# Seven products in place of eight for most of the second feed-forward matrix, with two weight sums made by DMA in DRAM

## The chip, the cores and the metric

One core of one Trainium2 chip runs the whole program. The metric is the device time of one execution in microseconds, the median of three runs. The profile was taken on one further execution of the same program.

## What is computed

Two encoder layers run over 512 prompt positions and 32 sample positions, 544 columns in all, in float32. Each layer has two feed-forward networks, and those hold most of the matrix work (model width 1024, inner width 2816):

```python
def swiglu(x, w_in, w_out):
    gate, up = jnp.split(x @ w_in, 2, axis=-1)
    return (jax.nn.silu(gate) * up) @ w_out
# in each layer, twice:
x = layer_norm(ALPHA * x + 0.5 * swiglu(x, w_ffn_in, w_ffn_out), ln_g, ln_b)
```

Between the two networks of a layer stands a mixer (pooling, a short convolution and attention) with an input and an output projection. There are four feed-forward networks in all; "first matrix" below is `w_ffn_in`, "second matrix" is `w_ffn_out`.

## The kernel before

**Layout.** Features lie on the 128 partitions, positions on the free axis. A vector of 1024 model features is 8 tiles of 128 x 544, the inner layer is 22 such tiles ("inner features"). The 544 positions are worked in two halves of 272 (`HS`), because a PSUM bank holds 512 float32 values.

**Three matmuls for one.** A float32 value is split into a high and a low part (`whi`, `wlo` for weights; `xh`, `xl` or `hh`, `hl` for activations). ScalarE copies the value to the high part (L172, L287), VectorE subtracts that from the value (L173, L288). One 128 x 128 block on one half then costs three matmuls of 272 columns: high by high, low by high, high by low.

**Weights.** The object `Weights` walks a list of units in the order in which TensorE needs them. SyncE loads a unit from DRAM into a `raw` buffer, ScalarE and VectorE split each stretch of up to 512 columns into a group (`whi`, `wlo`). There are 3 raw buffers of 1024 columns and 10 groups (`W_BUFS`). A group comes free when TensorE has done its last matmul with it, a raw buffer when the last split or sum that reads it is done.

**Seven products (Strassen's scheme in Winograd's form).** Of the first matrix, inner features 3 to 21 are worked by seven block products in place of eight: the blocks are (gate, up) by (first, second half of the model features), and on the other side the two halves of positions. `sums` (L201 to L216) loads four blocks of 128 x 512, makes four sums of them on VectorE (L198) and splits seven results. `Blocks.add` (L313) makes the sums on the activation side. `seven` (L330) runs 84 matmuls for such a unit; its seven products go to three banks in the order a b a c a c a, each followed by a step that reads the bank (`hidden`, L544). Inner features 0 to 2 are worked plainly with 96 matmuls.

**Second matrix.** The inner features are cut into parts of 8, 7 and 7 (`FSPLIT`). When a part's features are there (in truth one feature later, `plan`, L572), each of the 8 output tiles gets a plain product over the part (`mm2`), and `resid` (L444) adds the bank to `y`, once for each half. The last part runs in `out_phase` (L453), which also does the layer norm `LN`: GpSimd sums `acc` (L380, L381), takes a power (`rstd`, L412) and makes the low parts of the new activations (`xl`, L439). `start` (L521) begins the next network's first three units while the norm is still being applied.

**What sets the order.** A list scheduler puts each engine's instructions into one queue by program order, data and free buffers (the layer norm's steps are drawn forward by 300 places). On the chip every engine works through its own queue in that order and waits by semaphores. GpSimd's queue before holds only the layer norm's and the mixer's work: it has no DMA.

## Time and profile before

| | us |
|---|---|
| median of three runs | 2005.07 (2004.09 to 2005.29) |
| profiled execution | 2006.03 |
| its span, first to last instruction | 2004.2 |
| TensorE busy in the span | 1973.7 (98%) |
| VectorE busy | 1449.9 (72%) |
| ScalarE busy | 993.6 (50%) |
| GpSimd busy | 225.6 (11%) |

The span leaves out 1.8 us of the profiled execution, which lies 1.0 us above the median of the runs. The granted clock of TensorE is 0.992 of full speed over the span. The four feed-forward networks lie roughly at 6 to 383, 633 to 1008, 1012 to 1387 and 1626 to 2004 us. A matmul's busy time (288 ns) is longer than the distance between two matmuls, since they are pipelined; the distance is what counts.

### The profile page before, as it was taken

How to read it: one execution, taken by the hardware profiler on the slowest of the kernel's cores; microseconds unless marked ns; L12 is line 12 of the kernel's file. 1: busy time of each engine (PE TensorE's matmuls, PEld its weight loads, DVE VectorE, ACT ScalarE, POOL GpSimd, SP SyncE). 2: the span in 40 equal slices, each digit the busy share in tenths (PEclk: the TensorE clock that was granted, in tenths of full speed). 3: DMA queues.
4: the chain of work that ended last, by engine and by line, in shares of the span. 5: the costliest groups of instructions: out<-in, count | busy, mean ns of one | idle time of the engine just before them, and what ended most of it. 6: DMA issues, size and time to landing. Idle time of an engine off the chain costs nothing.

```text
span 2004.2 us, 38173 instructions
## 1 busy us (share of the span) xinstructions
PE 1973.7 (98%) x15446; PEld 1937.3 (97%) x15446; DVE 1449.9 (72%) x2806; ACT 993.6 (50%) x2000; POOL 225.6 (11%) x214
## 2 busy tenths in 40 slices
PE   9999999999999999999999999999999999999997
PEld 9999999999899999999999999999899999999997
DVE  7958677677658967768798496775865698576676
ACT  6625445465436544535466254454754366355453
POOL 0000000510134000000420000015001330000003
PEclk9999999999899999999999999999999999999999
DMA  6332323142121242323223223232421213323231
GB/s 208 113 102 95 99 83 116 64 144 92 59 81 63 87 123 67 116 85 102 89 73 108 85 93 109 85 106 72 140 98 54 85 50 99 106 85 109 89 98 46
DMA packets 65834, 189.12 MB, mean 94 GB/s; under 512 B 9428, under 2 KB 15188, under 8 KB 65656
## 3 DMA queue, kind: packets, MB, share of 16 engines
q1 hardware_dynamic: 55584, 172.07, 27.4%
q10 hardware_dynamic: 10072, 14.60, 2.3%
q8 instruction: 121, 1.98, 0.4%
q14 instruction: 57, 0.47, 0.1%
HBM read 179.88 MB, written 8.34 MB: 94 GB/s over the span
## 4 chain that ended last, share of the span: by engine, by line
PE 90%; DVE 6%; issue 1%; ACT 1%; DMA 1%; POOL 1%; POOLq 0%; ACTq 0%; DVEq 0%
PE b L341 39%; PE b L255 30%; PE b L259 15%; DVE wlo L173 1%; PE b L778 1%; PE b L777 1%; DVE sum L198 1%; PE b L793 1%; PE b L419 1%; DVE z L431 1%; ACT ya L433 1%; PE b L865 1%; PE b L758 0%; DMA raw<-in_w 0%; PE b L405 0%
## 5 line engine op out<-in xcount | busy, mean ns | idle before, releaser
L172 ACT ACTIVATE whi<-raw 128x512 fp32r<-128x512 f32 (+2 forms) x586 | 357.3, 614 | 495.6 <-PE b L259 299.1
L173 DVE TENSOR_TENSOR wlo<-raw,whi 128x512 fp32r<-128x512 f32 (+2 forms) x586 | 408.8, 700 | 149.0 <-ACT whi L172 144.2
L255 PE MATMUL b<-hh,wlo 128*128 128x272 f32 x1408 | 405.7, 288 | 0.0
L255 PE MATMUL b<-hh,whi 128*128 128x272 f32 x1408 | 405.1, 288 | 0.0
L259 PE MATMUL b<-hl,whi 128*128 128x272 f32 x1408 | 404.7, 287 | 0.0
L255 PE MATMUL b<-xh,whi 128*128 128x272 f32 x1024 | 296.3, 297 | 10.0 <-ACT xh L438 9.1
L172 ACT ACTIVATE whi<-sum 128x512 fp32r<-128x512 f32 x304 | 190.7, 631 | 201.4 <-PE b L259 99.5
L255 PE MATMUL b<-xh,wlo 128*128 128x272 f32 x1024 | 290.1, 290 | 0.1
L173 DVE TENSOR_TENSOR wlo<-sum,whi 128x512 fp32r<-128x512 f32 x304 | 207.8, 689 | 87.4 <-ACT whi L172 80.4
L259 PE MATMUL b<-xl,whi 128*128 128x272 f32 x1024 | 265.7, 290 | 0.0
L255 PEld LDWEIGHTS b<-hh,whi 128*128 128x128 f32 x1408 | 265.0, 188 | 0.0
L255 PEld LDWEIGHTS b<-hh,wlo 128*128 128x128 f32 x1408 | 264.9, 188 | 0.0
L259 PEld LDWEIGHTS b<-hl,whi 128*128 128x128 f32 x1408 | 264.9, 188 | 0.0
L341 PE MATMUL b<-xh,wlo 128*128 128x272 f32 x912 | 262.6, 288 | 0.0
L341 PE MATMUL b<-xh,whi 128*128 128x272 f32 x912 | 262.2, 288 | 0.0
L341 PE MATMUL b<-xl,whi 128*128 128x272 f32 x912 | 261.8, 287 | 0.0
L255 PEld LDWEIGHTS b<-xh,whi 128*128 128x128 f32 x1024 | 195.1, 191 | 14.0 <-ACT xh L438 11.7
L255 PEld LDWEIGHTS b<-xh,wlo 128*128 128x128 f32 x1024 | 195.5, 191 | 0.6 <-DVE wlo L173 0.3
L259 PEld LDWEIGHTS b<-xl,whi 128*128 128x128 f32 x1024 | 182.3, 190 | 0.7 <-issue 0.5
L341 PE MATMUL b<-s56h,whi 128*128 128x272 f32 x608 | 175.4, 289 | 3.3 <-ACT up L552 3.3
L388 POOL TENSOR_TENSOR ya<-ya,shift 128x544 f32<-128x544 f32 x14 | 25.3, 1830 | 1355.4 <-DVE wlo L173 1313.9
L341 PE MATMUL b<-s73h,wlo 128*128 128x272 f32 x608 | 175.3, 288 | 0.0
(208 smaller groups left out, 4248.1 us busy)
## 6 DMA issues: line engine op xcount, KB each, us to landing
raw<-in_w SPq DMA_DIRECT2D x184, 512.0 KB, 3.8
raw<-in_w SPq DMA_DIRECT2D x64, 448.0 KB, 3.3
raw<-in_wi SPq DMA_DIRECT2D x40, 512.0 KB, 3.2
raw<-in_w SPq DMA_DIRECT2D x42, 256.0 KB, 3.3
raw<-in_wo SPq DMA_DIRECT2D x16, 512.0 KB, 3.2
U<-scr ACTq DMA_DIRECT2D x8, 320.0 KB, 3.5
out_nkT<-k ACTq DMA_DIRECT2D x8, 272.0 KB, 2.1
out_nvT<-vT ACTq DMA_DIRECT2D x8, 272.0 KB, 2.2
```

What stands on the lines that cost most here:

```text
L172: S.activation(out=hi, in_=raw, func=AF.Copy)
L173: V.tensor_tensor(out=lo, in0=raw, in1=hi.bitcast(F32), op=ALU.subtract)
L198: V.tensor_tensor(out=r, in0=a, in1=b, op=ALU.add)
L255: PE.matmul(acc[:, :HALF], v, x[k][0][:, HS[h]], start=first and i == 0, stop=False)
L259: PE.matmul(acc[:, :HALF], w.at(k)[0], x[k][1][:, HS[h]], start=False, stop=last)
L341: PE.matmul(acc[:, :HALF], v[:, cs], x, start=opens and j == 0 and m == 0, stop=j == len(xs) - 1 and m == 2, skip_group_check=True)
L388: POOL.tensor_tensor(out=c, in0=c, in1=self.s, op=ALU.subtract)
L419: PE.matmul(b[:, c * CH:(c + 1) * CH], self.rstd[h][:, c:c + 1].to_broadcast([CH, P]), ident[:CH, :CH], start=True, stop=True)
L431: V.tensor_tensor(out=z, in0=c, in1=self.rstd[h], op=ALU.mult)
L433: S.activation(out=c, in_=z, func=AF.Identity, bias=b, scale=g)
L777: PE.matmul(g[:, :w], qc[c][parts[c], qs], kh[parts[c], :w], start=True, stop=False)
L778: PE.matmul(g[:, :w], qc[c][:, qs], kc[c][:, :w], start=False, stop=True)
```

## The change

The second matrix is now cut into parts of 6, 6, 4 and 6 inner features. The first three parts (16 of 22 features) are worked by seven products: the inner features of a part are taken in pairs (even, odd), the output tiles in pairs, the positions in halves. A unit of the second matrix is a pair of output tiles, with blocks of 384 columns (parts of 6) or 256 (the part of 4); it takes 63 or 42 matmuls in place of 72 or 48. Two such units run in turn, product by product (the `while pairs` loop). `resid7` adds each of the seven bank readings to `y`. Every pair of inner features now needs the activation sums of `Blocks.add`. The last part stays plain.

Of a unit's four weight sums, two (named r1 and r3) are made in DRAM: GpSimd issues a DMA that copies two neighbouring blocks into a DRAM buffer and a second DMA that adds two other blocks to it (`accum_op=ALU.add`). The buffers form a ring of 12; in the program's text the copy of a unit is issued 8 units ahead of the loading, the adding 4 units ahead, after a gate that waits for the first inner feature. This holds for all units of the first and the second matrix that are worked by seven products but the first two. SyncE then loads five blocks for a unit in place of four, now into 7 raw buffers of 512 columns. VectorE makes the two other sums.

In numbers, for the whole program: TensorE 15112 to 14728 matmul instructions; VectorE 2808 to 3364; ScalarE 2004 to 2278; GpSimd gains 244 DMAs (122 copies, 122 additions) and one small copy, the gate; SyncE's DMAs go from 384 to 872.

The tiles of the activations move, too: the first four model features and the even features of a part are held as two half tiles (pool tag `xh`, 16 buffers), and pool `xp` goes from 34 to 26 buffers. Two small loads of the bias go from SyncE's queue to ScalarE's. The core of the diff:

```diff
-FSPLIT = (8, 7, 7)
+FSPLIT = (6, 6, 4, 6)
+SUMS_AHEAD = (8, 4)
+SUMS_FROM = 2
-RAW_BUFS = 3
+RAW_BUFS = 7
         def load(self):
             kind, src, n = self.units[self.loaded]
             self.loaded += 1
+            self.sums_ahead()
...
+        def sums_ahead(self):
+            if self.gate is None:
+                return
+            for ahead, todo, step in zip(SUMS_AHEAD, self.todo, (self.copy, self.accumulate)):
+                while todo and todo[0] < self.loaded + ahead:
+                    step(todo.pop(0))
+
+        def copy(self, i):
+            _, src, n = self.units[i]
+            if len(self.ring) < SUMS_AHEAD[0] + 4:
+                t = dram.tile([P, 2 * G], F32, name=f"r13_{len(self.ring)}")
+            else:
+                t = self.ring.pop(0)
+            self.ring.append(t)
+            self.r13[i] = t[:, :2 * n]
+            with tc.issue_after(self.gate.ins):
+                POOL.dma_start(out=self.r13[i], in_=src[:, :2 * n])
+
+        def accumulate(self, i):
+            _, src, n = self.units[i]
+            POOL.dma_start(out=self.r13[i], in_=src[:, n:3 * n], accum_op=ALU.add)
...
-        def sums(self, src):
+        def seven(self, src, n, r13):
+            blocks = [src[:, :n], src[:, 3 * n:], src[:, 2 * n:3 * n]]
+            blocks += [src[:, n:2 * n]] if r13 is None else [r13[:, :n], r13[:, n:]]
+            b11, b21, b22, *b = (self.fetch(v) for v in blocks)
             g11, g21 = self.group(b11), self.group(b21)
-            r1 = self.add(b11, b12)
+            r1, r3 = b if b[1:] else (self.add(b11, b[0]), self.add(b[0], b22))
             r2 = self.add(r1, b22)
-            g2, g1 = self.group(r2), self.group(r1)
-            g3 = self.group(self.add(b12, b22))
-            g22 = self.group(b22)
+            g2, g1, g3, g22 = (self.group(v) for v in (r2, r1, r3, b22))
             return g11, g21, g2, g1, g3, g22, self.group(self.add(r2, b21))
...
+    def resid7(m, alpha):
+        seen = set()
+        def step(i, h, op):
+            def f(acc):
+                c = y[m + i][:, HS[h]]
+                if alpha and (i, h) not in seen:
+                    V.scalar_tensor_tensor(out=c, in0=c, scalar=ALPHA, in1=acc, op0=ALU.mult, op1=op)
+                else:
+                    V.tensor_tensor(out=c, in0=c, in1=acc, op=op)
+                seen.add((i, h))
+            return f
+        add, sub = ALU.add, ALU.subtract
+        return [step(0, 0, add), step(0, 0, add), step(1, 0, sub), step(1, 1, add), step(1, 1, sub), step(1, 0, add),
+                step(0, 1, add)]
...
-                hs.append(new_x("h"))
-                split(sg, hs[-1])
+                n = i - starts[last]
+                if n >= 0:
+                    tail.append(new_x("h") if n else new_b("h"))
+                    split(sg, tail[-1])
+                elif i % 2 == 0:
...
+                    hb.first.append(new_h("h", 1))
+                    split_half(sg, hb.first[-1], 0)
+                    held = sg
+                else:
+                    hb.second.append(new_x("h"))
+                    split(sg, hb.second[-1])
+                    hb.add(held, sg, new_x)
                 if i == 0:
+                    if W.gate is None:
+                        W.gate = POOL.tensor_copy(out=small("gate", 1), in_=sg[:, :1])
                     W.ahead(3)
...
-            for m in range(NK):
-                acc = run(mm2(W.get(), part, range(n)))
-                for h in range(2):
-                    resid(m, acc[h], h, i == 0)
+            for m in range(0, NK, 4):
+                pairs = [seven(W.get(), parts[i], resid7(m + j, i == 0)) for j in (0, 2)]
+                while pairs:
+                    pairs = [p for p in pairs if next(p, pairs) is not pairs]
```

**The order at two places.** First GpSimd, where the first layer's mixer ends and its second feed-forward network starts; `rstd` is the norm's power, once for each half, `xl` the low part of an activation tile. Before:

```order
L381 TENSOR_TENSOR acc_7261<-acc_7261,sq 128x544 [waits Activation_49,Pool_49]
L412 TENSOR_TENSOR rstd<-var,mhalf 68x4 [waits DVE_49]
L439 TENSOR_TENSOR xl<-ya,xh 128x272 [waits PE_49,Activation_49] x8
L412 TENSOR_TENSOR rstd<-var,mhalf 68x4 [waits DVE_49]
L439 TENSOR_TENSOR xl<-ya,xh 128x272 [waits Activation_49] x8
L388 TENSOR_TENSOR ya<-ya,shift 128x544 [waits DVE_49,Activation_49]
```

After, at the same place (`r_5` is slot 5 of the DRAM ring, L219 the copy, L223 the addition; the DMAHW semaphores are those of loads from SyncE's and ScalarE's queues, the DMASW ones those of GpSimd's own DMAs):

```order
L458 TENSOR_TENSOR rstd<-var,mhalf 68x4 [waits DVE_49]
L485 TENSOR_TENSOR xl<-ya,xh 128x272 [waits PE_49,Activation_49] x8
L458 TENSOR_TENSOR rstd<-var,mhalf 68x4 [waits DVE_49]
L219 DMA r_5_453<-in_w 128x1024 [waits DMAHW1_49,DMAHW0_49]
L485 TENSOR_TENSOR xl<-ya,xh 128x272 [waits Activation_49] x4
L223 DMA r_5_453<-in_w 128x1024 [waits DMASW3_49,DMASW2_49]
L485 TENSOR_TENSOR xl<-ya,xh 128x272 [waits Activation_49]
L485 TENSOR_TENSOR xl<-ya,xh 128x272
L485 TENSOR_TENSOR xl<-ya,xh 128x272 [waits Activation_49] x2
L219 DMA r_6_598<-in_w 128x1024 [waits DMAHW6_49,DMAHW5_49]
L223 DMA r_6_598<-in_w 128x1024 [waits DMASW5_49,DMASW4_49]
```

Between the second power and the eight `xl` of the second half there now stand a copy and an addition; behind them copies and additions alternate, a copy waiting for the loads that last read its ring slot, an addition for its copy. Second, VectorE where the first stretch of the second matrix begins (`ya` is the residual, `sum` a weight sum). Before:

```order
L288 TENSOR_TENSOR hl<-sg,hh 128x544 [waits Activation_49]
L449 SCALAR_TENSOR_TENSOR ya<-ya,b 128x272 [waits PE_49]
L173 TENSOR_TENSOR wlo<-raw,whi 128x512 [waits DMAHW1_49,Activation_49]
L449 SCALAR_TENSOR_TENSOR ya<-ya,b 128x272 [waits PE_49]
L173 TENSOR_TENSOR wlo<-raw,whi 128x512 [waits Activation_49]
L449 SCALAR_TENSOR_TENSOR ya<-ya,b 128x272 [waits PE_49]
L198 TENSOR_TENSOR sum<-raw 128x512 [waits DMAHW4_49]
L173 TENSOR_TENSOR wlo<-raw,whi 128x512 [waits DMAHW2_49,Activation_49]
```

After:

```order
L636 SCALAR_TENSOR_TENSOR ya<-ya,b 128x272
L183 TENSOR_TENSOR wlo<-sum,whi 128x384 [waits Activation_49]
L227 TENSOR_TENSOR sum<-raw 128x384 [waits DMAHW7_49,DMAHW6_49]
L638 TENSOR_TENSOR ya<-ya,b 128x272 [waits DVE_49]
L183 TENSOR_TENSOR wlo<-raw,whi 128x384 [waits DMAHW4_49,Activation_49]
L227 TENSOR_TENSOR sum<-sum,raw 128x384 [waits DMAHW5_49,DVE_49]
L183 TENSOR_TENSOR wlo<-raw,whi 128x384 [waits Activation_49]
L638 TENSOR_TENSOR ya<-ya,b 128x272
L636 SCALAR_TENSOR_TENSOR ya<-ya,b 128x272
L183 TENSOR_TENSOR wlo<-sum,whi 128x384 [waits Activation_49]
```

Additions to the residual, splits and weight sums now alternate in one queue, with fourteen residual additions for two units.

## Rows read from the trace of the kernel before

**Rows 1.** Page, busy us of each engine, share, instructions.

```profile
PE 1973.7 (98%) x15446; PEld 1937.3 (97%) x15446; DVE 1449.9 (72%) x2806; ACT 993.6 (50%) x2000; POOL 225.6 (11%) x214
```

**Rows 2.** Page, chain that ended last: shares by engine.

```profile
PE 90%; DVE 6%; issue 1%; ACT 1%; DMA 1%; POOL 1%; POOLq 0%; ACTq 0%; DVEq 0%
```

**Rows 3.** Waits, core 0: us in total, times, longest.

```profile
PE b L255 <- ACT xh L438: 9.1, 10, 2.1
...
PE b L419 <- POOL rstd L412: 5.3, 7, 2.0
...
ACT whi L172 <- PE b L341: 264.6, 444, 1.4
...
DVE sum L198 <- DMA raw<-in_w: 33.4, 16, 2.9
```

**Rows 4.** Timeline of TensorE, 330 us: start, length, operation.

```profile
330.01 0.29 PE L341 MATMUL b<-s56h,wlo 128*128 128x272 f32 x1
...
332.90 0.29 PE L341 MATMUL b<-s73h,whi 128*128 128x272 f32 x1
```

**Rows 5.** Windows: stretch, length, busy (instructions) of each engine, PEclk, DMA share, GB/s.

```profile
170.00:210.00 40.00, 40.00 (x322) 40.00 (x321) 36.49 (x66) 24.38 (x45) 0.00 (x0) 1.00 0.32 97
...
230.00:270.00 40.00, 40.00 (x323) 40.00 (x322) 21.66 (x42) 9.79 (x17) 0.00 (x0) 1.00 0.28 89
...
20.00:100.00 80.00, 79.82 (x628) 78.27 (x627) 74.30 (x144) 53.92 (x101) 0.00 (x0) 1.00 0.43 130
...
640.00:1000.00 360.00, 356.40 (x2849) 355.46 (x2848) 269.19 (x485) 174.93 (x324) 21.61 (x16) 1.00 0.31 94
...
10.00:20.00 10.00, 10.00 (x82) 10.00 (x81) 6.65 (x20) 6.04 (x18) 0.00 (x0) 1.00 0.97 305
```

**Rows 6.** Groups by form, VectorE: busy, mean ns | idle before.

```profile
L173 DVE TENSOR_TENSOR wlo<-raw,whi 128x512 fp32r<-128x512 f32 x510 | 365.0, 718 | 138.6 <-ACT whi L172 136.0
...
L173 DVE TENSOR_TENSOR wlo<-raw,whi 128x384 fp32r<-128x384 f32 x64 | 38.9, 608 | 9.9 <-ACT whi L172 7.9
...
L173 DVE TENSOR_TENSOR wlo<-raw,whi 128x256 fp32r<-128x256 f32 x12 | 4.8, 420 | 0.5 <-ACT whi L172 0.4
...
L198 DVE TENSOR_TENSOR sum<-raw 128x512 f32<-128x512 f32 x152 | 106.3, 699 | 17.0 <-DMA raw<-in_w 14.8
...
L451 DVE TENSOR_TENSOR ya<-ya,b 128x272 f32<-128x272 f32 x108 | 46.7, 432 | 32.5 <-PE b L259 32.0
...
L288 DVE TENSOR_TENSOR s56l<-s,s56h 128x544 fp32r<-128x544 f32 x16 | 11.4, 713 | 0.0
...
L319 DVE TENSOR_TENSOR s<-ya,s 128x272 f32<-128x272 f32 x16 | 6.9, 429 | 0.0
```

**Rows 7.** Page, queues and DMA issues: KB each, us to landing.

```profile
q1 hardware_dynamic: 55584, 172.07, 27.4%
...
raw<-in_w SPq DMA_DIRECT2D x184, 512.0 KB, 3.8
...
scr<-rows ACTq DMA_DIRECT2D x1, 1536.0 KB, 8.7
```

**Rows 8.** Timeline around 630 us: GpSimd, VectorE, TensorE.

```profile
628.56 1.39 POOL L412 TENSOR_TENSOR rstd<-var,mhalf 68x4 f32<-68x4 f32 x1 [0.71 <-DVE var L411]
...
633.14 7.88 POOL L439 TENSOR_TENSOR xl<-ya,xh 128x272 fp32r<-128x272 f32 x8 [3.19 <-ACT xh L438]
...
628.40 0.68 DVE L198 TENSOR_TENSOR sum<-raw 128x512 f32<-128x512 f32 x1
...
633.94 1.26 DVE L198 TENSOR_TENSOR sum<-sum,raw 128x512 f32<-128x512 f32 x1
...
641.51 0.91 PE L259 MATMUL b<-xl,whi 128*128 128x272 f32 x6
```

**Rows 9.** Timeline of ScalarE's queue, 31 us: issue of a DMA.

```profile
31.66 0.63 ACTq L629 DMA_DIRECT2D scr<-rows  x1
```

More of the change, by code (lines that the diff above doesn't have):

```diff
@@ L81, in encoder_kernel @@
     w2: bass.AP,
+    w2t: bass.AP,
     wi: bass.AP,
@@ L163, in __init__, with fetch @@
             self.units, self.used, self.loaded, self.ready = units, 0, 0, []
-        def fetch(self):
-            return wp.tile([P, 2 * G], F32, tag="raw", name="raw", bufs=RAW_BUFS)
+            self.r13, self.ring, self.gate = {}, [], None
+            self.todo = [[i for i, u in enumerate(units) if u[0] == "s"][SUMS_FROM:] for _ in range(2)]
+        def fetch(self, src):
+            raw = wp.tile([P, G], F32, tag="raw", name="raw", bufs=RAW_BUFS)[:, :src.shape[-1]]
+            nc.sync.dma_start(out=raw, in_=src)
+            return raw
         def new_group(self):
@@ L436, in scale @@
                 return
[L437 to L439 removed]
+            xh, xl = (self.x[k].at(i, h) for i in range(2))
+            S.activation(out=xh, in_=c, func=AF.Copy)
+            POOL.tensor_tensor(out=xl, in0=c, in1=xh.bitcast(F32), op=ALU.subtract)
         def apply(self, h, k):
@@ L491, in out_phase @@
         if not ln.final:
-            ln.x = [new_x("x") for _ in range(NK)]
+            ln.x = new_xs()
         g = tail_mm(1, 1)
@@ L560, in c12 @@
             times(up, h0)
-        seven(ws, blocks, [
+        run(seven(ws, blocks, [
             copy(up),
@@ L569, in hidden @@
             lambda acc: times(acc, h1),
-        ])
+        ]))
         return sg
     def plan():
-        ends = [sum(FSPLIT[:s + 1]) for s in range(len(FSPLIT))]
+        ends = [sum(FSPLIT[:s + 1]) for s in range(len(FSPLIT) - 1)]
         for i in range(NF):
@@ L580, in plan @@
         yield 2, len(FSPLIT) - 1
+    def resid7(m, alpha):
[12 more added lines that the diff above has]
+                step(0, 1, add)]
     def ffn(l, f, x, pre):
-        xb = Blocks(x)
-        hs = []
+        xb = Blocks(x[:NK // 2], x[NK // 2:])
+        last = len(FSPLIT) - 1
+        starts = [sum(FSPLIT[:s]) for s in range(last + 1)]
+        parts, tail = [], []
         for what, i in plan():
@@ L1033, in encoder_kernel @@
     W = Weights(units)
-    x = [new_x("x") for _ in range(NK)]
+    x = new_xs()
     warm = bank()
```

125 lines of the change are left out of this document (66 added, 59 removed).

## Prediction

> **What bounds the kernel now.** I read the page's busy times first: TensorE is busy 1973.7 of 2004.2 us, VectorE 72%, ScalarE 50%, GpSimd 11% [rows 1]. The chain that ended last says the same from the other side: 90% of it is TensorE [rows 2]. TensorE's own waits are small; the two largest sum to 9.1 and 5.3 us, both at the layer norms, while ScalarE waits 264.6 us for TensorE to give weight groups free [rows 3]. So weights are made ahead of need, and the bound is the number of matmuls times their distance.
>
> The distance: 23 matmuls start between 330.01 and 332.90 us [rows 4], 0.1257 us each, with granted clock 1.00. A first-matrix unit (84 matmuls) takes 10.56 us, a second-matrix unit with 384 columns (63) 7.92 us, one with 256 (42) 5.28 us.
>
> The averages hide one thing. In a stretch of first-matrix units VectorE is busy 36.49 of 40 us (91%), in a stretch of the second matrix 21.66 of 40 (54%) [rows 5]. The change takes matmuls out of the second kind of stretch and puts VectorE's work in.
>
> **TensorE: 48.3 us less.** 15112 matmuls become 14728. 384 x 0.1257 = 48.3 us, all of it on the path, as the engine has no idle time to absorb it. This is the most the change can bring by its own idea.
>
> **VectorE: more work, and where.** From the instruction counts and the rows by form [rows 6]: splits of 512 columns, 96 fewer x 0.718 = -69; of 384, 160 more x 0.608 = +97; of 256, 144 more x 0.420 = +60; weight sums of 512, 148 fewer x 0.699 = -103; of 384 and 256 (no row; I take the split of the same width) 64 x 0.608 + 32 x 0.420 = +52; residual additions 208 x 0.432 = +90; activation sums 128 x 0.429 = +55; activation splits 32 x 0.713 + 32 x 0.432 = +37. Together +219 us, 1450 to 1669, 85% of a span near 1971. Per network +55: the window of the second one held 269 of 360 us [rows 5] and would hold 324 of 348.
>
> By kind of unit: a first-matrix unit needs 0.912 x 10.56 = 9.63 us of VectorE now. Two weight sums go (-1.40). Per pair of features come four activation sums and two splits, less half a split: 4 x 0.429 + 2 x 0.713 - 0.28 = 2.86, so 1.43 per unit. It comes to 9.66, unchanged, under 10.56: no cost, with 0.9 us to spare. A second-matrix unit with 384 columns needs 9 x 0.608 (seven splits, two sums) + 7 x 0.432 = 8.50 us against TensorE's 7.92; one with 256 needs 9 x 0.420 + 3.02 = 6.80 against 5.28. Four units in turn are over by 2.3 us (384) or 6.1 us (256). What covers this is the lead: ten weight groups, two of them in use, so eight products, 8 x 9 x 0.1257 = 9.0 us at 384 columns and 8 x 6 x 0.1257 = 6.0 us at 256. The stretches of 384 are covered; that of 256 just is or isn't. Bounds: 0 with the whole lead, 4 x (2.3 + 2.3 + 6.1) = 43 us with none. I take 2 us per network, **8 us**, near the lower end, because ScalarE's waits for TensorE show that the lead is there.
>
> **The first network's start.** From 20 to 100 us VectorE is busy 74.30 of 80 us [rows 5]. Three pairs of features add 3 x 2.86 = 8.6 us, and only one unit there already saves its 1.4 us, since the first two units still make all their sums on VectorE: 81.5 us in 80. Bounds 1.5 us (all idle time used) to 7.2 us (none); I take **4 us**.
>
> **GpSimd's queue at the norms.** At three entries to a network a copy and an addition stand between the second `rstd` and the eight `xl`. Now `xl` runs from 633.14 to 641.02, 0.98 us each, and TensorE uses the last ones from 641.51 on [rows 8]: under 1 us of slack. The copy waits for the load that last read its ring slot. That load can start when the splits ahead of the norm's scaling are done (628.4, where VectorE has already gone on to a sum) and lands 3.8 us later [rows 7, 8]: about 632.2. Issuing a DMA has no row on GpSimd; the nearest are 0.63 us for ScalarE's issue of a copy from DRAM to DRAM [rows 9] and 1.39 for a small operation of GpSimd. With 0.63 the first `xl` is not late. After four `xl` (637.1) the addition waits for its copy. The one such copy in the trace, 1536 KB, landed after 8.7 us [rows 7]; a third of the bytes lies between 2.9 and 8.7, so it is there at 635 to 641.5, and the last four `xl` are 0.6 to 5 us late. Three entries: 0 to 15 us, I take **3 us** (it is nearer to 512 KB in 3.8 us).
>
> **DMA.** SyncE's queue took 27.4% of 16 engines for 172.07 MB [rows 7], 51 engine-us per MB. A first-matrix unit will load five blocks (1.31 MB, 67 engine-us), copy 0.52 MB (27) and add 0.52 MB: 27 if an addition moves like a copy, 54 if it costs double. That is 121 to 148 of 16 x 10.56 = 169, against 0.32 now [rows 5]. The engines have been at 0.97 with 305 GB/s [rows 5], so this can run. The Trainium skill ("Collectives: The Full Stack", the section on the fold count) says that an adding DMA is slower because it reads two sources, about half of a copy's rate; by that the upper figure, 88% busy, would hold, and no run here shows it yet. Loads will land later than 3.8 us. I cost this at nothing: sums are ready up to 12 units ahead, and the seven raw buffers turn over once in 1.4 units. VectorE's wait for loads, 33.4 us [rows 3], may grow; TensorE feels that only when the lead is used up. ScalarE's extra work (some 100 us on 994) and SyncE's extra issues lie beside the matmuls too.
>
> **Sum.** 2005.1 - 48.3 + 8 + 4 + 3 = 1972 us, 1.7% less. (The profiled execution: 2006.0 - 33.3 = 1972.7; it lies 1.0 above the median.)
>
> **Rivals.** *A: VectorE becomes the bound in the second matrix's stretches.* For it: 107 and 129% by the count above, and a queue in which a residual addition stands behind splits. Against it: the lead. If none of the excess is covered, 1956.8 + 43 = 2000 us; by degrees 1988 to 2003.
>
> *B, the slower one: GpSimd's DMAs hold up VectorE.* While GpSimd ran its eight `xl`, a weight sum on VectorE took 1.26 us, alone 0.68 [rows 8]: VectorE loses 0.46 of the time in which GpSimd works. Before, GpSimd works 226 us in all; now it issues 61 DMAs per network. If issuing one holds VectorE like such an operation for d us, VectorE loses 61 x 0.46 x d = 28d per network, against the 24 us that it has free (348 - 324). The kernel gets slower than before when the loss passes 24 + 33/4 = 32 us, that is d = 1.15 us. At d = 1.5: 4 x (42 - 24) = 72 us, 2044 us. For it: the row, and that an operation of GpSimd takes 0.98 us and more. Against it: nothing shows that issuing reads what VectorE reads. The Trainium skill ("SBUF — State Buffer", "Who interferes with whom") says that a VectorE operation with two SBUF inputs contends with a GpSimd instruction that reads SBUF, not with one that only writes, and takes descriptor generation to be a writer. By that rule, d = 0 and B falls away; the contention of `xl` agrees with its first half (1.26 against 0.68).
>
> *C: the sums in DRAM come too late,* so that the change doesn't do what it says. SyncE's queue is in order: a load that waits for an addition holds up all loads behind it. A network has 31 such units in some 348 us. Were an addition four times a copy (107 engine-us), the network would need 19 x 201 + 8 x 151 + 4 x 100 engine-us plus 322 for its plain units, 5750 / 16 = 359 us: four times 11 us above, 2016 us. The turning point against before is near an addition of 3.6 copies.
>
> **How the numbers follow.** Forecast 1972 us (own range 1956 to 1988), chance 0.64. A 0.17, B 0.11, C 0.08. No change means within 0.2%, 2001 to 2009, about what a measurement of this kernel can tell. Faster: 0.64 + 0.14 of A = 0.78. Same: 0.03 of A, 0.03 of B and C = 0.06. Slower: 0.16, the rest of B and C. The range starts at 1955, just below the pure saving (1957), and goes to 2004, taking in A's whole excess and leaving out the slower cases.
>
> **What would show it.** Right: TensorE's distance still near 0.126 us and its busy time about 48 us less; VectorE near 1670 us; TensorE's waits on `wlo` or on residual additions some 10 to 15 us, most of them in the 256-column stretches and before 110 us. A is right if those waits reach 30 us or more. B is right if splits of 512 columns average well above 0.718 us where GpSimd issues. C is right if SyncE's queue waits on GpSimd's DMAs. The forecast is wrong if TensorE's idle time, 30 us now, passes 65.

## The result, and the profile after

The changed kernel takes 2108.5 us (2106.3 to 2111.1), the kernel before beside it 2004.6: a ratio of 1.0518, 95% interval 1.0503 to 1.0534. Forecast were 1972 us and a range of 1955 to 2004. The miss is 136 us, and the sign is wrong too.

The page of the changed kernel: busy times, then the granted clock and the DMA share in 40 slices, then the shares of the chain that ended last.

```profile
PE 1983.8 (94%) x15062; PEld 1934.4 (92%) x15062; DVE 1602.9 (76%) x3362; ACT 1095.9 (52%) x2272; POOL 386.3 (18%) x459
...
PEclk9899999999999999999999999999999999999997
DMA  9987887323222687888347878862431237766331
...
PE 61%; DVE 17%; DMA 14%; issue 5%; ACT 2%; POOL 1%; DVEq 0%; ACTq 0%; POOLq 0%; SPq 0%
```

TensorE is idle for 121 us (2104.9 - 1983.8) where it was 30 [rows 1]. Its busy time did not fall by the 48 us of the 384 matmuls saved but rose by 10. The grant is lower: 0.968 over the span, where it was 0.992, and below full in several slices; on some 1925 us of matmuls (1973.7 - 48.3) that is about 48 of the missing 58 us, by my estimate. The chain, 90% TensorE before [rows 2], now runs for 14% through DMAs.

The queues, and the loads' median time from issue to landing (KB each, us):

```profile
q1 hardware_dynamic: 126048, 199.79, 30.9%
q0 software_dynamic: 32064, 111.16, 25.0%
...
r<-in_w POOLq DMA_DIRECT2D x148, 512.0 KB, 6.9
raw<-in_w SPq DMA_DIRECT2D x272, 256.0 KB, 4.5
raw<-r SPq DMA_DIRECT2D x148, 256.0 KB, 4.7
```

GpSimd's queue (q0) is new. A load of 256 KB now takes longer, 4.5 to 4.7 us, than one of twice the bytes took before (3.8 [rows 7]). Three stretches show where (the first two are those of [rows 5], the third lies inside its 640 to 1000 us; the DMA share is the last figure but one):

```profile
20.00:100.00 80.00, 67.60 (x495) 64.36 (x495) 59.85 (x124) 44.20 (x86) 18.40 (x28) 0.94 0.98 265
170.00:210.00 40.00, 39.87 (x320) 39.66 (x319) 36.55 (x76) 25.54 (x49) 6.04 (x9) 1.00 0.72 188
700.00:1000.00 300.00, 284.84 (x2206) 281.62 (x2206) 247.40 (x514) 164.84 (x321) 39.44 (x58) 0.98 0.80 204
```

From 20 to 100 us the DMA engines are 98% busy (0.43 before), and 495 matmuls run where 628 ran. From 170 to 210 us the share is 0.72 and TensorE is busy nearly throughout. From 700 to 1000 us the share is 0.80, before it was 0.31, and 2206 matmuls run; the run without GpSimd's DMAs, below, has 2292 there. Who waits (us in total, times, longest):

```profile
POOL r L223 <- DMA r<-in_w: 601.9, 112, 10.4
...
DVE sum L227 <- DMA raw<-r: 148.7, 66, 7.8
...
PE b L386 <- DVE ya L638: 29.0, 16, 5.4
PE b L386 <- DVE sg L613: 23.2, 14, 3.5
PE b L451 <- DVE acc L441: 13.4, 7, 3.1
```

VectorE waits 149 us at the first sum of a unit that it makes, which needs the load of r1, where its wait for loads at its sums was 33.4 [rows 3]. TensorE then waits for VectorE: for residual additions (`ya`) and products (`sg`) that stand behind that sum in VectorE's queue. One instance, from the timelines of GpSimd, SyncE's queue, VectorE and TensorE (start, length, operation, idle time before it and what ended it):

```profile
210.40 0.54 POOL L219 DMA_DIRECT2D r<-in_w  x1 [0.21 <-issue]
212.88 2.63 SPq L175 DMA_DIRECT2D raw<-r  x2
218.59 0.81 POOL L223 DMA_DIRECT2D r<-in_w  x1 [7.65 <-DMA r<-in_w]
219.78 0.56 DVE L227 TENSOR_TENSOR sum<-raw 128x384 f32<-128x384 f32 x1 [4.21 <-DMA raw<-r]
220.72 0.43 DVE L638 TENSOR_TENSOR ya<-ya,b 128x272 f32<-128x272 f32 x1
...
221.30 0.36 PE L386 MATMUL b<-hh,whi 128*128 128x272 f32 x1 [1.71 <-DVE ya L638]
```

GpSimd's copy is issued at 210.40 and is done 8 us later (at 218.59 starts the addition, which had waited for it). The two loads that SyncE issues from 212.88 fall into that time, and the sum that needs one of them starts only at 219.78, after 4.21 us of idle VectorE. The residual addition behind it (`ya`, 220.72) sets a bank free that TensorE has awaited for 1.71 us.

### The profile page after: what moved, and what is told of

It is laid out like the page before. It is cut to its first block, busy times and chain, and to the rows that moved or that the text cites. A ratio compares the mean times of both kernels' runs of the same rounds, so it can differ in the third digit from the quotient of the medians.

```text
span 2104.9 us, 40402 instructions
## 1 busy us (share of the span) xinstructions
PE 1983.8 (94%) x15062; PEld 1934.4 (92%) x15062; DVE 1602.9 (76%) x3362; ACT 1095.9 (52%) x2272; POOL 386.3 (18%) x459
## 3 DMA queue, kind: packets, MB, share of 16 engines
q1 hardware_dynamic: 126048, 199.79, 30.9%
q0 software_dynamic: 32064, 111.16, 25.0%
## 4 chain that ended last, share of the span: by engine, by line
PE 61%; DVE 17%; DMA 14%; issue 5%; ACT 2%; POOL 1%; DVEq 0%; ACTq 0%; POOLq 0%; SPq 0%
PE b L386 32%; PE b L279 15%; DMA raw<-r 13%; PE b L283 7%; DVE wlo L183 7%; DVE sum L227 2%; DVE ya L638 2%; PE b L857 1%; PE b L856 1%; ACT whi L182 1%; PE b L872 1%; DVE s56l L334 1%; ACT ya L479 1%; PE b L465 1%; DVE s73l L334 1%
## 5 line engine op out<-in xcount | busy, mean ns | idle before, releaser
L182 ACT ACTIVATE whi<-raw 128x512 fp32r<-128x512 f32 (+2 forms) x846 | 479.3, 577 | 443.6 <-PE b L386 310.2
L183 DVE TENSOR_TENSOR wlo<-raw,whi 128x512 fp32r<-128x512 f32 (+2 forms) x846 | 540.6, 648 | 82.5 <-ACT whi L182 76.5
L386 PE MATMUL b<-s73h,whi 128*128 128x272 f32 x864 | 256.6, 297 | 26.2 <-DVE ya L638 12.5
L386 PE MATMUL b<-s73l,whi 128*128 128x272 f32 x864 | 254.2, 294 | 0.0
L386 PE MATMUL b<-s56h,wlo 128*128 128x272 f32 x864 | 250.0, 289 | 0.0
L386 PE MATMUL b<-s56l,whi 128*128 128x272 f32 x864 | 249.0, 289 | 0.1
L182 ACT ACTIVATE whi<-sum 128x512 fp32r<-128x512 f32 (+2 forms) x252 | 144.9, 576 | 174.7 <-PE b L386 101.7
L223 POOL DMA_DIRECT2D r<-in_w x122 | 99.2, 813 | 664.2 <-DMA r<-in_w 601.9
L279 PEld LDWEIGHTS b<-xh,whi 128*128 128x128 f32 x1024 | 194.8, 191 | 15.3 <-ACT xh L484 12.6
L386 PEld LDWEIGHTS b<-xh,whi 128*128 128x128 f32 x912 | 176.7, 194 | 28.1 <-DVE sg L613 27.2
L386 PEld LDWEIGHTS b<-s73h,whi 128*128 128x128 f32 x864 | 169.2, 196 | 28.6 <-DVE ya L638 13.4
```

Source lines behind the costliest of these rows:

```text
L182: S.activation(out=hi, in_=raw, func=AF.Copy)
L183: V.tensor_tensor(out=lo, in0=raw, in1=hi.bitcast(F32), op=ALU.subtract)
L223: POOL.dma_start(out=self.r13[i], in_=src[:, n:3 * n], accum_op=ALU.add)
L279: PE.matmul(acc[:, :HALF], v, x[k].at(0, h), start=first and i == 0, stop=False)
L386: PE.matmul(acc[:, :HALF], v[:, cs], x, start=opens and j == 0 and m == 0, stop=j == len(xs) - 1 and m == 2, skip_group_check=True)
```

## Experiments

I put three theories beside each other. **D**: the load of GpSimd's DMAs makes SyncE's loads land late. **V**: VectorE is the bound (rival A). **C**: the sums come too late (rival C). Two more came up on the way: **T**, the last group of six features, and the place or number of raw loads.

### No sums in DRAM; no GpSimd DMAs; DMAs that nobody reads; half the change

All weight sums on VectorE:

```diff
-SUMS_FROM = 2
+SUMS_FROM = 1000
```

> The changed kernel with every weight sum back on VectorE: no copy and no addition in DRAM, four loads of a block a unit instead of five, seven products for the second matrix kept. Theory D (GpSimd's copies and additions, 111 MB, fill the DMA engines in the feed-forward stretches to a share of 0.7 to 1.0, so SyncE's loads of raw blocks land late and VectorE waits for them 149 us): that wait falls below 40 us although VectorE has 244 more sums of 0.6 to 0.7 us (busy 1603 to about 1755 us), TensorE's idle time of 121 us falls below 60, and the time is 1985 to 2025 us. Theory V (VectorE cannot keep up with the second matrix by seven products, with its seven evacuations a pair and its sums of the features): 150 us more work on VectorE makes it worse than the changed kernel, 2120 us or more.

No copy and no addition, the five loads kept:

```diff
-            blocks += ... [r13[:, :n], r13[:, n:]]
+            blocks += ... [src[:, n:2 * n], src[:, :n]]
...
-                POOL.dma_start(out=self.r13[i], in_=src[:, :2 * n])
...
-            POOL.dma_start(out=self.r13[i], in_=src[:, n:3 * n], accum_op=ALU.add)
+            pass
```

> The changed kernel without the copies and additions in DRAM; SyncE still loads five blocks a unit, but the fourth and fifth come straight from the weights (left out: the two sums r1 and r3, so two of the seven products have a plain block in place of a sum). VectorE's instructions, the five loads a unit and the seven slots stay. Theory D: without the 111 MB the loads land as before, VectorE's wait for them falls below 40 us, the time is 1960 to 1990 us. Theory L (five loads a unit in seven slots with VectorE's order putting the first sum on the fourth load is too little lead, whoever else uses the DMA engines): the wait stays above 100 us and the time above 2070 us. Theory C (the sums in DRAM come too late): also 1960 to 1990, since nothing waits for a sum; the next run tells C from D.

Copies and additions made but not read (the first two lines of that diff alone):

> The copies and additions in DRAM are made as in the changed kernel, but nobody reads them: SyncE loads the fourth and fifth block straight from the weights (left out: the sums r1 and r3 in the products). Same DMA traffic, no dependence on GpSimd's sums. Theory D (load on the DMA engines and the memory): 2080 to 2120 us, VectorE's wait for raw blocks stays above 100 us. Theory C (the sums are late): 1960 to 1995 us and a wait below 40 us, although the DMA share stays at about 0.59 of the span.

The first half of the change alone, on the second matrix of before:

```diff
-FSPLIT = (6, 6, 4, 6)
+FSPLIT = (8, 7, 7)
...
-                pairs = [seven(W.get(), parts[i], resid7(m + j, i == 0)) for j in (0, 2)]
+                acc = run(mm2(W.get(), part, range(n)))
```

> Half of the change alone: the kernel before with its second matrix, but with r1 and r3 of the first matrix (76 units less two) made in DRAM by GpSimd's copy and addition, loads of 512 columns in seven slots. Theory D: the first-matrix stretches carry the same DMA load as in the changed kernel and VectorE waits there for raw blocks, 40 to 100 us in all; the time is 2020 to 2070 us, slower than the 2004.6 of the kernel before. Theory V (the second matrix is at fault): 1995 to 2006 us.

Measured: 2015.7, 2002.6, 2230.2 and 2041.4 us. The first and the fourth lie in the range that D gave and far from V's, so V is not the main cause. The second is 12 us above D's range and the third 110 us above, for reasons shown below. Taking GpSimd's DMAs away while the five loads stay gives back 106 us (2108.5 to 2002.6); giving VectorE 244 sums more, which by V should cost, gives back 93, and its wait at the sums falls to 0.7 us. Page and waits of the run without GpSimd's DMAs:

```profile
PE 1955.5 (98%) x15062; PEld 1911.1 (95%) x15062; DVE 1602.3 (80%) x3362; ACT 1096.0 (55%) x2272; POOL 223.4 (11%) x215
...
raw<-in_w SPq DMA_DIRECT2D x420, 256.0 KB, 3.4
...
DVE sum L224 <- DMA raw<-in_w: 43.9, 42, 2.2
```

Loads of 256 KB land after 3.4 us instead of 4.5 to 4.7, VectorE waits 44 us instead of 149 (above the 40 that I had set), and TensorE is idle for 47.5 us instead of 121 and busy for 28 us less. These two differences, 73.6 and 28.3, are the 102 us between the two profiled spans.

The third run missed: I expected no more than 2120 us and got 2230. Unread, a sum has no ring slot to wait for, so GpSimd was held back by nothing and sent all 244 DMAs in the first 605 us, within the first network. Two stretches of that run, during and after:

```profile
20.00:600.00 580.00, 399.72 (x2731) 389.63 (x2729) 300.68 (x620) 201.10 (x389) 179.60 (x256) 0.84 1.02 264
1260.00:1560.00 300.00, 297.35 (x2353) 295.47 (x2353) 260.77 (x539) 174.39 (x339) 0.00 (x0) 1.00 0.40 121
```

During them the DMA share is full and TensorE is busy for 400 of 580 us at a granted clock of 0.84; the first network ends at 603.6 us instead of 374.7, which is the whole 228 us between these two runs. After them 2353 matmuls run in 300 us; the run without GpSimd's DMAs has 2356 in a stretch of that kind. So the same kernel, with nobody waiting for a sum, loses all its time beside the DMAs and none without them. It is a harsher load than the changed kernel's, not the same one, so it shows the direction and not the size.

The fourth run, with the first matrix alone, has a wait above the 40 to 100 us that I expected, though its loads land little later than without GpSimd's DMAs:

```profile
raw<-r SPq DMA_DIRECT2D x148, 256.0 KB, 3.6
...
DVE sum L226 <- DMA raw<-r: 122.1, 56, 5.2
```

A median hides the late loads: of the loads of 256 KB straight from `in_w` every tenth takes 6.7 us or more there, 8.1 in the changed kernel and 4.1 without GpSimd's DMAs. And the wait costs little by itself. From the ends of the networks (as in the table below) this run loses 24 us against the kernel before in the first one and 7, 4 and 2 in the others, with VectorE waiting 18 to 40 us in each. There VectorE is busy for 67% of the span, and in the second matrix, plain as in the kernel before, it has time to catch up (54% busy [rows 5]). That late loads cost 19 to 24 us a network in the changed kernel may thus need its fuller queue on VectorE as well; no run separates that from its greater number of GpSimd DMAs.

### Sums earlier, half the bytes

```diff
-SUMS_AHEAD = (8, 4)
+SUMS_AHEAD = (18, 12)
```

> The changed kernel with the sums begun earlier: the copy 18 units ahead instead of 8, the addition 12 instead of 4, the ring in DRAM 22 entries instead of 12. Theory C (sums late: SyncE's loads of r1 and r3 wait for the additions): VectorE's wait of 149 us falls below 60, the time to 2010 to 2040 us. Theory D: the same bytes, only more of them at once at the start of a network: 2095 to 2130 us, the wait stays above 120 us.

2125.5 us, and the wait grew to 165.1 us: C falls. Of the wait, 15.4 us are one instance at 77 us, where SyncE stood 15.0 us for the first addition. The first network alone is 24 us longer than in the changed kernel, the second 5, the third is equal and the fourth 15 us shorter, for a reason that stays open. C falls in the trace of the changed kernel too: matched in order, each addition has landed at least 13 us before the load of its sum is issued, and from the fourth on at least 35 us before.

```diff
-                POOL.dma_start(out=self.r13[i], in_=src[:, :2 * n])
+                POOL.dma_start(out=self.r13[i], in_=src[:, :n])
...
-            POOL.dma_start(out=self.r13[i], in_=src[:, n:3 * n], accum_op=ALU.add)
+            POOL.dma_start(out=self.r13[i], in_=src[:, n:2 * n], accum_op=ALU.add)
...
-            blocks += ... [r13[:, :n], r13[:, n:]]
+            blocks += ... [r13, src[:, n:2 * n]]
```

> The changed kernel with copies and additions of half the width: only r1 is made in DRAM, and the fifth block is loaded straight from the weights (left out: the sum r3 in one product of seven). The same number of DMAs on GpSimd's queue and the same waits, half the bytes (55.6 MB for 111.2). Theory D by bytes (engines and memory near full): most of the 106 us between the changed kernel and the one without these DMAs goes, 2010 to 2045 us, since the share in feed-forward stretches falls from 0.9 to about 0.65. If the price is one for each DMA or each wait in GpSimd's chain, not for its bytes: 2080 us or more.

2068.2 us, between the two expectations: half the bytes give back 40 of 106 us (34 and 47 in its two executions, of 2074.5 and 2061.9 us). The four networks tell the two parts of the price apart. From the starts of `rstd` in GpSimd's timeline, each network from the second `rstd` of the norm ahead of it (the first from 0) to the first of its own (for half the bytes from the slower execution):

| us | 1 | 2 | 3 | 4 |
|---|---|---|---|---|
| without GpSimd's DMAs | 374.7 | 359.6 | 361.3 | 353.9 |
| half the bytes | 392.1 | 377.9 | 379.6 | 368.7 |
| the changed kernel | 415.5 | 378.8 | 383.1 | 377.8 |

In the first network, where the copies of the start come at once (share 0.98 from 20 to 100 us, 0.88 with half the bytes), the price is 41 us with all bytes and 17 with half. In the others it is 19 to 24 and 15 to 18, at shares of 0.80 and 0.63 from 700 to 1000 us. Of the 65 us of these three networks half the bytes give back 14, or up to 26 if the 12.6 us between the two executions all lay there: less than half. So the bytes alone don't set the price there. What stays is that a GpSimd DMA is nearly always under way: a unit has two, one after the other, of 5.3 us each at half width and 6.9 at full, and TensorE's part of a unit is 10.6 us. That this is why each load lands late is argued from these figures; no run separates it from the number of DMAs, nor tells whether loads wait at the DMA engines or at the memory behind them.

### Number, order and lead of the raw loads

```diff
-W_BUFS = 10
-RAW_BUFS = 7
+W_BUFS = 9
+RAW_BUFS = 9
```

> The changed kernel with nine slots for raw blocks instead of seven, and nine instead of ten for the split weights (to make room). If VectorE's wait comes from loads that are issued only when a slot comes free and then take 4.7 us, two more slots let SyncE issue two loads earlier, some 2 to 4 us: the wait of 149 us falls below 90 and the time to 2030 to 2080 us. If the engines' bandwidth is what is short (share near 0.9), a longer lead gains nothing: 2095 to 2120 us.

2153.3 us. The room for the two slots came from the split weights, so a control was needed, with `W_BUFS = 9` alone:

> Control for the run with nine raw slots, which took 2153.3 us: the changed kernel with nine slots for the split weights instead of ten and the seven raw slots that it has. If the ninth and tenth slot of the split weights were what that run lost: 2130 to 2170 us here too, and two more raw slots bought nothing. If more loads in flight were what it lost: 2100 to 2115 us.

2153.1 us: the lost slot of split weights is the whole 45 us, and two more raw slots brought nothing that shows (the two executions with them lie 26 us apart). The split weights are the lead that hides late loads, and in the changed kernel there is none to spare; what a slot is worth without GpSimd's DMAs was not run.

```diff
+                blocks = [blocks[i] for i in (2, 3, 0, 1, 4)]
+                b22, r1, b11, b21, r3 = (self.fetch(v) for v in blocks)
```

> The changed kernel with the five loads of a unit in another order: the two that VectorE's first sum adds (the fourth block and r1) come first and second, instead of third and fourth. If the 149 us that VectorE waits at that sum are a matter of the load's place in SyncE's order, the wait falls below 60 us and the time to 2060 to 2085 us. If every load of the unit is late by as much (the engines shared with GpSimd's DMAs), the wait moves to the split of the blocks that now come last and the time stays at 2095 to 2120 us.

2231.3 us, far above either number. The wait did move, as the second theory has it, to what now comes late, but it did not leave the sum either. Its waits:

```profile
DVE sum L227 <- DMA raw<-r: 155.7, 64, 7.0
...
DVE sum L227 <- DMA raw<-in_w: 94.2, 49, 6.6
...
ACT whi L182 <- DMA raw<-in_w: 70.0, 40, 6.3
```

The first two products need the two blocks that now are loaded third and fourth. The given order is the better one. The waits now lie at loads of every kind, which fits loads that are all late and not r1's alone; but the new order brings waits of its own, so the run doesn't prove it.

### The last group beside the norm

The run without GpSimd's DMAs still took 2002.6, 30 us above the forecast. One number of the kernel before, changed:

```diff
-FSPLIT = (8, 7, 7)
+FSPLIT = (8, 8, 6)
```

> The kernel before with one number changed: the second matrix in groups of 8, 8 and 6 inner features instead of 8, 7 and 7, so that the last group, whose products run beside the norm at each network's end, has 6 as in the changed kernel. The number of matmuls stays. Theory T (the run without any of GpSimd's DMAs still took 2002.6 us instead of the 1972 that I predicted because the shorter last group ends before GpSimd's two accumulations a block, some 1.4 us each, so TensorE idles about 3 us on the last of them and then runs some 10 us at its lower clock): 2020 to 2035 us, TensorE's wait on the accumulated sums rises from 1.4 to about 13 us and the granted clock falls below 1 behind each network. The rival (those 30 us are VectorE's, from seven evacuations a pair): 2003 to 2007 us, no change.

2035.3 us, a ratio of 1.0156 (1.0136 to 1.0176), with the same number of matmuls. T holds (0.3 us above its range). TensorE's wait in the kernel before and in this run, then the end of the first network in this run's timelines of GpSimd, VectorE and TensorE, with the granted clock (third figure from the end) of the 20 us behind it, and last the stretch at the same place in the kernel before:

```profile
PE b L405 <- DVE acc L395: 1.4, 3, 1.0
...
PE b L405 <- DVE acc L395: 13.2, 7, 3.1
...
374.89 1.33 POOL L381 TENSOR_TENSOR acc<-acc,sq 128x544 f32<-128x544 f32 x1
374.97 1.55 DVE L395 TENSOR_TENSOR acc<-acc,ya 128x272 f32<-128x272 f32 x1 [1.19 <-POOL acc L380]
377.84 0.73 PE L405 MATMUL b<-onesd,acc 128*68 128x1 f32 x8 [3.06 <-DVE acc L395]
380.72 0.43 PE L255 MATMUL b<-hh,wlo 128*128 128x272 f32 x1
380.94 0.43 PE L259 MATMUL b<-hl,whi 128*128 128x272 f32 x1
...
380.00:390.00 10.00, 8.52 (x40) 8.20 (x39) 5.31 (x17) 3.45 (x8) 1.02 (x1) 0.58 0.00 0
390.00:400.00 10.00, 9.05 (x65) 8.93 (x66) 9.46 (x22) 6.66 (x18) 6.76 (x8) 0.83 0.17 54
...
375.00:385.00 10.00, 7.66 (x56) 7.22 (x56) 9.14 (x26) 6.70 (x15) 2.84 (x4) 0.96 0.14 52
```

A block of the last group now takes 4.5 us of matmuls instead of 5.3, and they are over before the norm's sums are: GpSimd starts its last accumulation at 374.89, VectorE, which waited for GpSimd, its first at 374.97, and TensorE stands still for 3.06 us until they are done. Then two matmuls are 0.22 us apart instead of 0.1257, and the granted clock of the next 10 us is 0.58: most of them at the lower of the two levels (1.2 GHz). In the kernel before it was 0.96 from 375 to 385 us. Waits and clock together make up the loss: 11.8 us more of waiting, and a grant of 0.982 over the span where it was 0.992, which by my estimate is some 20 us of 2034. The changed kernel has the same wait (`acc`, 13.4 us above).

Both causes removed at once, no GpSimd DMAs and groups of 6, 4, 4 and 8:

> The changed kernel without GpSimd's copies and additions (fourth and fifth block loaded straight from the weights; left out: the sums r1 and r3) and with groups of 6, 4, 4 and 8, so that the group beside the norm has 8 features. If the miss of my prediction is the DMA load and the short last group and nothing else, what is left is the prediction's own sum: 1972 us plus 6 us for 48 matmuls that are no longer saved, 1972 to 1985 us, with TensorE idle for 25 to 35 us. If VectorE is a third cause (80% busy): 1995 us or more.

1974.6 us, a ratio of 0.9836 (0.9809 to 0.9862), and TensorE idle for 32 us of a span of 1971.9:

```profile
PE 1939.7 (98%) x15110; PEld 1896.3 (96%) x15110; DVE 1575.0 (80%) x3338; ACT 1083.3 (55%) x2264; POOL 226.6 (11%) x215
```

So the forecast's own arithmetic holds once these two are out of the way: 1972 plus 6 for fewer features gives 1978. As a version it is no use, since it leaves the two sums out.

### VectorE, and a version that beats both

With all sums on VectorE and a last group of 8 (`FSPLIT = (6, 4, 4, 8)`, `SUMS_FROM = 1000`):

> The changed kernel with all weight sums on VectorE as in the run of 2015.7 us, and the second matrix in groups of 6, 4, 4 and 8 instead of 6, 6, 4 and 6: the last group has 8 features, and 14 of 22 instead of 16 go by seven products (48 matmuls fewer saved, +6.0 us at 0.1257 us each). Theory T: the longer last group covers the norm, 25 to 30 us come back, less 6: 1990 to 1998 us, and TensorE's wait on the accumulated sums is 2 us or less. The rival (VectorE, 85% busy, is what costs): 2015 to 2025 us.

2011.4 us, between the two expectations: `acc` is down to 1.4 us, but only 4 us came back. Here V is right. The stretch from 100 to 320 us of this run, then of the run without GpSimd's DMAs and with the same groups (fourth figure: VectorE's busy time):

```profile
100.00:320.00 220.00, 213.72 (x1673) 209.91 (x1672) 213.72 (x460) 120.64 (x249) 0.00 (x0) 1.00 0.33 100
100.00:320.00 220.00, 219.41 (x1741) 218.13 (x1741) 196.28 (x414) 129.03 (x258) 0.00 (x0) 1.00 0.43 130
```

VectorE is busy for 213.7 of 220 us and TensorE starts 1673 matmuls; with 196.3 it starts 1741. The 68 matmuls are 8.5 us, in one of four networks. With part of the sums in DRAM, every third unit (`[SUMS_FROM::3]`) and every second:

> Groups of 6, 4, 4 and 8, and only every third of the units has r1 and r3 made in DRAM, the others all four sums on VectorE. About a third of the bytes of GpSimd's queue (37 MB for 111) against a third of the sums (some 80 of 244, 50 us of VectorE). If the price of DMA load grows faster than its bytes (the engines' share in these stretches 0.35 without, 0.5 with a third, 0.9 with all): 1985 to 2000 us, faster than before's 2004.6 and than the 2011.4 with all sums on VectorE. If each unit that loads r1 and r3 from DRAM pays the same 0.85 us (106 us over 124 units): 35 us are paid for some 30 gained, 2010 to 2020 us.

> As the run before, with every second unit's sums in DRAM (about 56 MB, 122 sums taken from VectorE). If the price grows faster than the bytes: 1990 to 2010 us; if it is 0.85 us a unit: 2015 to 2030 us.

2024.6 and 2032.3 us: my first expectation was wrong twice, and both lie just above the second. By network the run with a third is 15.7 us slower than the one with none in the first (397.7 against 382.0), 0.3 faster and 1.0 slower in the second and third and 3.4 faster in the fourth. Spread thin, the DMAs pay for themselves at best; the first network's start does not bear them.

What is left is to give VectorE less. Only one group by seven products (6 of 22 features), then two:

```diff
-FSPLIT = (6, 6, 4, 6)
+FSPLIT = (6, 8, 8)
+NSEVEN = 1
...
-SUMS_FROM = 2
+SUMS_FROM = 1000
...
+            if i >= NSEVEN:
+                for m in range(NK):
+                    acc = run(mm2(W.get(), parts[i], range(FSPLIT[i])))
```

> No sums in DRAM (all four on VectorE), second matrix in groups of 6, 8 and 8, of which only the first goes by seven products (6 features of 22, 144 matmuls saved, 18 us at 0.1257 us each). Theory V for what is left without GpSimd's DMAs and with a long last group (2011.4 us with 14 features by seven, 1974.6 where VectorE is spared two sums a unit: VectorE is at 95 to 100% in the feed-forward stretches): each feature by seven costs VectorE some 4.1 us a network, so 6 instead of 14 leave it idle time, TensorE keeps its gain, and the time is 1983 to 1995 us, faster than the kernel before. If the loss lies elsewhere (the start of the first network, 6 us later than before in that run, or loads of 512 columns): 2000 to 2012 us.

> As the run before with groups of 6, 4, 4 and 8, of which the first two go by seven products (10 features, 240 matmuls saved, 30 us), the third as before. Theory V: between the run with 6 and the one with 14; VectorE has some 66 us less to do than there: 1985 to 2003 us. If the loss lies elsewhere: 2003 to 2012 us.

1997.5 us (ratio 0.9955, 0.9939 to 0.9971) and 2002.9 (0.9985, 0.9976 to 0.9995): of 14, 10 and 6 features by seven products (2011.4, 2002.9, 1997.5) fewer is better, as V has it, though the run with 6 lies 2.5 us above its range. Its first network ended 6 us later than before's. With the group by seven products second, where VectorE has caught up (`FSPLIT = (8, 6, 8)`, `SEVEN = (1,)`):

> No sums in DRAM, groups of 8, 6 and 8 inner features, of which the second goes by seven products (6 of 22, as in the run of 1997.5 us, where it was the first). In that run the first network ended 6 us later than before's, since VectorE, 100% busy from 50 to 110 us with the sums of the features, could not also serve the seven products that came at 50 to 100 us; the other networks took 3.8 to 5.1 us less than before's. If that is so, the later group gives the 6 us back: 1987 to 1994 us. If the first network's loss is its loads or its start: 1996 to 1999 us as there.

1991.6 us, a ratio of 0.9933 (0.9921 to 0.9946): faster than both kernels. VectorE from 50 to 110 us, with the group first and with the group second:

```profile
50.00:110.00 60.00, 55.16 (x399) 52.81 (x398) 57.94 (x119) 32.19 (x66) 0.00 (x0) 0.95 0.31 93
50.00:110.00 60.00, 60.00 (x480) 59.88 (x479) 53.78 (x100) 36.96 (x72) 0.00 (x0) 1.00 0.42 124
```

57.9 of 60 us busy and 399 matmuls against 53.8 and 480; the first network ends at 373.0 instead of 382.1 us. The control for its last group of 8, the kernel before with 7, 7 and 8:

> Control for every run with a last group of 8: the kernel before with groups of 7, 7 and 8, nothing by seven products in the second matrix. If the gain of the run with 8, 6 and 8 (or 6, 8 and 8) is that of the seven products: 2002 to 2006 us, no change. If it is only the longer last group's cover of the norm (the shorter one of 6 cost 31 us): 1990 to 1999 us.

2003.4 us, 0.9994 (0.9985 to 1.0003), no difference: the gain is that of the seven products, 12 to 13 of the 18 us that 144 matmuls are worth.

## Why the prediction was wrong, step by step

- **TensorE, 48.3 us less: right.** The distance is still 0.1257 us at full clock; of the 42.2 us that 336 fewer matmuls are worth in the run without both causes, 32.3 us arrived (2004.2 to 1971.9 between the profiled spans). In the changed kernel the saving is there and is buried.
- **VectorE, +219 us: too much.** Its busy time rose by 153 us (1449.9 to 1602.9 [rows 1]). The counts and durations were right: the durations of all its instructions, added up, rose by 222 us (1582.8 to 1804.6), and the 512-column splits average 719 ns (718 before [rows 6]), the 384-column ones 554 (608). But neighbours overlap, as below, where two operations start 0.47 us apart and the first lasts 0.55; the overlaps grew from 133 to 202 us. Durations added up overstate a busy engine's time.

```profile
223.17 0.55 DVE L183 TENSOR_TENSOR wlo<-raw,whi 128x384 fp32r<-128x384 f32 x1
223.64 0.43 DVE L638 TENSOR_TENSOR ya<-ya,b 128x272 f32<-128x272 f32 x1
```

- **Second-matrix excess, first network's start and norm queue, 8 + 4 + 3 us: right in size.** Without both causes the cost beside the matmuls is 42.2 - 32.3 = 10 us. By network the saving falls short of its 10.6 us by 5, 3, 3 and 1 us (ends of the networks, as in the table above), near the forecast's 6 in the first and 2 in each other. The sign that I had set for it doesn't show, though: TensorE's waits on `wlo` and on residual additions are 1.5 us there, not 10 to 15. So the size and the network are right, while what TensorE loses there is open. TensorE's wait on `rstd` is 4.7 us in the changed kernel (5.3 [rows 3]) and no wait on `xl` shows, so the 3 us for GpSimd's queue were nearer to none.
- **DMA, "I cost this at nothing": the step that failed, 106 us.** The traffic was worked out rightly at 121 to 148 engine-us of 169. SyncE's queue took 52.1 engine-us per MB (30.9% of 16 x 2104.9 over 199.79 MB), GpSimd's 75.7 (25.0%, 111.16 MB): near the upper end. The Trainium skill ("Collectives: The Full Stack", the section on the fold count) has the adding transfers of a ReduceScatter at about half of a copy's rate, since each reads two sources; with copies at 52 the additions would be at 99 by my estimate, which agrees, though no run timed them apart. What I drew from it was wrong: that engines which can run at 0.97 may run at 0.88 at no cost. The median time to landing of a 256 KB load rose by a third (3.4 to 4.5 and 4.7 us). I wrote that VectorE's wait may grow and that TensorE feels it only when the lead is used up, and did not work out when that is: in the changed kernel one slot of split weights in ten is worth 45 us.
- **The last group, 7 to 6 features: missing, 31 to 34 us.** `FSPLIT`'s last number stood in the diff, and I counted only matmuls by it. The group also sets how long TensorE covers GpSimd's accumulation ahead of each norm. One number of before changed gives 31 us. The two runs without GpSimd's DMAs give 28 (1974.6 to 2002.6); the run with the short last group has two more features by seven products, worth 6 us, so the group's own price there is 34.
- **Sum.** 1972 + 31 to 34 + 106 = 2109 to 2112 us; measured 2108.5. The 106 and the 34 are differences along one chain of runs, so of these only the 31 checks the sum independently.
- **Rival A** would have been called right by the sign that I gave it: TensorE's waits on residual additions and `wlo` reached 42.5 us (29.0 + 8.5 on additions, 5.0 on `wlo`). That sign was a bad one. VectorE stood idle for a load just ahead of such an addition in the instance above, and without the DMAs the wait on `sg` was 4.3 us and on `ya` 1.0. A's mechanism, VectorE as the bound, showed only where VectorE makes all the sums.
- **Rival B** is out: splits of 512 columns did not slow (719 ns). GpSimd's issues take 0.59 us (copy) and 0.81 us (addition); the 78 splits that overlap one average 686 ns, as do the 432 beside no work of GpSimd, while the 52 beside its other operations take 1046. The rule of the Trainium skill that I set against B ("SBUF — State Buffer", "Who interferes with whom") agrees with that.
- **Rival C** has the sign (2016 us forecast) but neither the size nor the reason: in the changed kernel SyncE's queue shows no wait on GpSimd's DMAs, and earlier sums were slower.
- The limit that I had set, TensorE idle for more than 65 us, was passed (121), and the chances (slower 0.16) were far too low, since only an engine's throughput and no load's latency stood among the rivals.

## What to carry to other kernels

Work moved from a compute engine to DMAs isn't free because the DMA engines have room: ask what the loads on the critical queue then take from issue to landing, and how many of them the buffers behind can hide. When a list of sizes changes, look for everything that runs beside the piece whose size changed; here one feature fewer in the last group cost 31 us, two thirds of what all the saved matmuls were worth. A new algorithm that trades TensorE for VectorE pays only up to VectorE's idle time, stage by stage: 6 features of 22 gained, 14 lost.

## What the runs showed of the hardware that I had not expected

- Loads of 256 KB landed after 3.3 us (median, all sums on VectorE), 3.7 to 4.0 with half of GpSimd's bytes and 4.5 to 4.7 with all, at DMA shares of 0.33, 0.63 and 0.80 from 700 to 1000 us. The Trainium skill ("DMA: Bandwidth & Descriptors", "Issuing engines are not separate DMA queues") says that DMAs from all issuing engines run on the same 16 engines and interleave there; the landing times agree.
- Half the bytes cost more than half of what all of them cost outside the first network (15 to 18 against 19 to 24 us in the profiled executions). The Trainium skill ("DMA: Bandwidth & Descriptors", "Queues, rings and completion order") says that each engine takes a packet from one queue, then from the next; that would make a load wait for a packet of the other queue however few there are. No run here shows it.
- A pause of 3.06 us on TensorE was followed by 10 us with a granted clock of 0.58, and 0.83 in the next 10. Waits of 13.2 us in all (1.4 in the kernel before) came with 31 us more of time.
- Unheld, GpSimd's 244 DMAs kept the DMA engines full for 580 us (a share of 1.02, 264 GB/s), and TensorE was busy for 69% of that time, at a granted clock of 0.84.
